# One layer of a hybrid encoder step: gate projections by seven products, gate and branch projections with the tokens stationary

## The chip, the core and the metric

The kernel runs on one core of one Trainium2 chip, as one launch. The metric is the device time of one execution in microseconds (us), median of several. Besides there is one profiled execution, whose trace and profile page are quoted here. Engines are named as in the profile: PE is TensorE (matmuls), DVE is VectorE, ACT is ScalarE, POOL is GpSimd, SP is SyncE; the last two mostly issue DMAs here.

## What is computed

384 tokens (256 of a new prompt, 8 x 16 of running streams) go through one layer with model width 2048; all is fp32.

```
u = rmsnorm(x);  P = u @ w_in            # columns: pool 2048 | z 4096 | x,B,C 6144 | dt 64 | gates a, b 2 x 2048
A = pooled(P.pool) per group @ pool_w * pool_scale      # windows 2, 4, 8, 16: mean minus self
B = gated_rmsnorm(ssd_scan(silu(conv(x,B,C)), dt) + D x, silu(z))
m = sigmoid(g_a) * (A @ w_pool_proj) + sigmoid(g_b) * (B @ w_ssd_proj)
x = x + rmsnorm(m @ w_out)
x = x + rmsnorm(relu(rmsnorm(x) @ w_up)^2 @ w_down)
```

New pool, conv and SSD states are outputs too.

## The kernel before

Every fp32 operand of a matmul is split into a high part (`h`, rounded to the short fp32 format of TensorE) and the rest (`l`); a product is then three matmuls, h by h, l by h and h by l, into one PSUM accumulator (`mm3`, L80 to L82). The split of a weight tile of 128 x 1024 is one ACT copy (L71) and one DVE subtraction (L73); activations are split in the same way. SP fetches the weight tiles (`wfetch`, L63, 512 KB each) into three buffers.

Most projections are written with the weights stationary: a tile of 128 output columns stays in the array and the 384 tokens move, so one matmul has 384 columns and the result lies with features on partitions and tokens along the free axis. `proj` runs over the k-tiles of such a tile, 16 for the input projections (`xgh`, `xgl`, the split normalised input without its per-token factor `rstd`), 32 for the SSD projection. The output projection `wo` and the MLP's down projection are written the other way (`moving`, `down_units`): 128 tokens are stationary, 512 weight columns move, and the result has tokens on partitions. The down projection already computes the 256 prompt tokens by Strassen's seven products over 2 x 2 blocks (tokens by k by columns) and the 128 stream tokens plainly; `down_units` forms the sums of weight blocks on DVE (L862), evicts its accumulators by ACT copies (L878), and adds them up in DRAM by accumulating POOL DMAs (L882).

The order of the work is that of the program text, except for the MLP, whose units are put in order by `run`:

1. Input tiles p0 to p15 of the pool branch (`pool_tile`: windows by shifted additions on DVE, L251), with the group maps (`pool_map`) between them.
2. Gate a and the pool product, tile by tile: `gate_a(n)`, then `proj` of `w_pp`, their product to DRAM (`ma_scr`). `dt_phase` stands behind the last map: a chain of small DVE and ACT instructions with its transposes (`tk`).
3. Eight SSD groups: six `conv` tiles, four z tiles, the scan's matmuls (its C by B product is `cb`, L461), results to DRAM (`a_scr`). After each of the first six groups comes one tile of gate b (`gate_b`), after the last group the other ten; each goes to DRAM (`gb_scr`).
4. The SSD projection, tile by tile over 32 k-tiles, with `a_scr` read back through three buffers (`ar`, L617) and split (`abh` L620, `abl` L621); the merged tile is formed with `ma_scr` and `gb_scr` (`mar`, `gbr`) and split into `mh`, `ml`.
5. `wo` (L652 to L654), second norm, MLP up and down.

PSUM has eight banks, four for `mmtile` and four for `sstile`, all through.

Of the kernel before, what the change touches and what calls it, by code (L numbers as in the profile page):

```python
# [17 lines left out]
NB = 8  # L18
# [9 lines left out]
NG = 6  # L28
# [6 lines left out]
def build(ctx, tc, io):  # L35
# [5 lines left out]
    psm = ctx.enter_context(tc.tile_pool(name="psm", bufs=4, space=PSUM))  # L41
    pss = ctx.enter_context(tc.tile_pool(name="pss", bufs=4, space=PSUM))
    dram = ctx.enter_context(tc.tile_pool(name="dram", bufs=1, space=DRAM))

    cst = consts.tile([P, 352], F32, name="cst")
    vec = consts.tile([P, V_END], F32, name="vec")
# [3 lines left out]
    def mmtile(name):  # L50
        return psm.tile([P, 512], F32, tag="mm", name=name)

    def sstile(name):
        return pss.tile([P, 512], F32, tag="ss", name=name)

    hold = [None, None]
# [4 lines left out]
    def wfetch(src, name):  # L61
        w = wpool.tile([P, 1024], F32, tag="w", name=f"w_{name}")
        sy.dma_start(w, src)  # L63
        return w, name

    def wsplit(f):
        w, name = f
        h = wpool.tile([P, 1024], F32R, tag="wh", name=f"wh_{name}")
        l = wpool.tile([P, 1024], F32R, tag="wl", name=f"wl_{name}")
        with behind(hold[0]):  # L70
            s.activation(h, w, AF.Copy)  # L71
        with behind(hold[1]):
            v.tensor_tensor(l, w, h.bitcast(F32), ALU.subtract)  # L73
        return h, l
# [16 lines left out]
    last = [None]  # L91

    def proj(units, rhs, name):
        o = mmtile(f"pj_{name}")[:, :T]
        for q, src in enumerate(units):
            half(o, q, wload(src, f"{name}_{q}"), rhs)
        return o
# [15 lines left out]
    def rms_bc(pool, sumsq, n, name, after=None):  # L113
# [5 lines left out]
        y = newton(pool, ms, [P, 3], name)  # L119
        dg = pool.tile([P, 3, P], F32, tag="dg", name=f"dg_{name}", bufs=1)  # L120
# [8 lines left out]
    ma_scr = [dram.tile([P, T], F32, name=f"ma_scr{i}") for i in range(16)]  # L129
    gb_scr = [dram.tile([P, T], F32, name=f"gb_scr{i}") for i in range(16)]  # L130
# [3 lines left out]
    dec_scr = dram.tile([NH, NB], F32, name="dec_scr")  # L134

# [37 lines left out]
    w = wpool.tile([P, 1024], F32, tag="w", name="w_p0_0")  # L173
# [37 lines left out]
    s.copy(rstd, rms_bc(pa, acc, DM, "x"))  # L211
    pha.close()

    small.tile([P, 88], F32, name="pad_small")
    tok = small.tile([P, 11, NH], F32, name="tok")
    decb = small.tile([P, NH, NB], F32, name="decb")
    with tc.tile_pool(name="phc", bufs=1, reuse_waits="tile") as pc, tc.tile_pool(name="phc2", bufs=2, reuse_waits="tile") as pc2:
        pst = pc.tile([P, KD, NB, 15], F32, name="pst")
        gp.dma_start(pst, io["state_pool"])
        bufs = []  # L220
        for i in range(2):
            b = pc.tile([P, 519], F32, name=f"pbuf{i}")
            gp.memset(b[:, :15], 0.0)
            bufs.append(b)
        A = [None] * KD
        dd = [[None] * 4 for _ in range(4)]

        def pool_tile(gi, k4):
            w = WINDOWS[gi]
            k = gi * 4 + k4  # L230
            ps = early[k] if k < 3 else proj(in_units(1 + k), xg, f"p{k}")
            bf = bufs[k % 2]
            pv = bf[:, 15:271]
            sv = bf[:, 271:].rearrange("p (b t) -> p b t", b=NB)
# [7 lines left out]
            s.copy(sv[:, :, :15], pst[:, k])  # L242
# [10 lines left out]
            d = pc2.tile([P, T], F32, tag="d", name=f"d{k}")  # L253
            v.scalar_tensor_tensor(
# [13 lines left out]
            h = pc2.tile([P, T], F32R, tag=f"dh{k4}", name=f"dh{k}", bufs=1)  # L268
            l = pc2.tile([P, T], F32R, tag=f"dl{k4}", name=f"dl{k}", bufs=1)
            s.activation(h, d, AF.Copy)  # L270
            v.tensor_tensor(l, d, h.bitcast(F32), ALU.subtract)
            dd[gi][k4] = (h, l)

        def pool_map(gi):
            for hf in range(2):
                h, l = wload(io["pool_w"][gi, hf], f"pw{gi}_{hf}")
                for n2 in range(2):
                    n = gi * 4 + hf * 2 + n2
                    o = mmtile(f"pw{n}")[:, :T]
                    for k in range(4):  # L280
                        c = slice((n2 * 4 + k) * P, (n2 * 4 + k + 1) * P)
                        mm3(o, h[:, c], l[:, c], dd[gi][k][0], dd[gi][k][1], k == 0, k == 3)
                    ah = pc.tile([P, T], F32R, name=f"ah{n}")
                    al = pc.tile([P, T], F32R, name=f"al{n}")
                    sc = vec[:, V_PSC + n : V_PSC + n + 1]
                    s.activation(ah, o, AF.Copy, scale=sc)
                    v.scalar_tensor_tensor(
                        out=al, in0=o, scalar=sc, in1=ah.bitcast(F32), op0=ALU.mult, op1=ALU.subtract
                    )
                    A[n] = (ah, al)  # L290

        def gate_a(n):
            ps = proj(in_units(17 + n), xg, f"ga{n}")
            t = pc2.tile([P, T], F32, tag="d", name=f"gat{n}")
            v.tensor_tensor(t, ps, rstd, ALU.mult)
            sg = pc2.tile([P, T], F32, tag="sg", name=f"gas{n}")
            s.activation(sg, t, AF.Sigmoid)
            return sg

        def dt_phase(pb):  # L300
            ps = proj(in_units(0), xg, "dt")
            n64 = lambda nm: pb.tile([NH, T], F32, name=nm)
            dtb = vec[:NH, V_DTB : V_DTB + 1]
            alog = vec[:NH, V_ALOG : V_ALOG + 1]
            nA = pb.tile([NH, 1], F32, name="nA")
            s.activation(nA, alog, AF.Exp)
            raw, ab, e, t1, t2, q = (n64(x) for x in ("raw", "ab", "e", "t1", "t2", "q"))
            v.tensor_tensor(raw, ps[:NH], rstd[:NH], ALU.mult)
            s.activation(ab, raw, AF.Abs, bias=dtb)
            s.activation(e, ab, AF.Exp, scale=-1.0)  # L310
            v.tensor_scalar(t1, e, 2.0, None, ALU.add)
            v.reciprocal(t2, t1)
            v.tensor_tensor(t1, e, t2, ALU.mult)
            v.tensor_tensor(t2, t1, t1, ALU.mult)
            v.tensor_scalar(q, t2, 1.0 / 19.0, None, ALU.mult)
            for i in range(8, 0, -1):
                v.scalar_tensor_tensor(out=q, in0=q, scalar=1.0 / (2 * i + 1), in1=t2, op0=ALU.add, op1=ALU.mult)
            v.scalar_tensor_tensor(out=q, in0=q, scalar=1.0, in1=t1, op0=ALU.add, op1=ALU.mult)
            v.tensor_scalar(raw, raw, dtb, 0.0, ALU.add, ALU.max)
            dt, cum = n64("dt"), n64("cum")  # L320
            v.scalar_tensor_tensor(out=dt, in0=q, scalar=2.0, in1=raw, op0=ALU.mult, op1=ALU.add)
            dta, we, dtw = n64("dta"), n64("we"), n64("dtw")
            v.tensor_scalar(dta, dt, nA, -1.0, ALU.mult, ALU.mult)
            v.tensor_tensor_scan(cum, cst2[:NH, C_SCAN - C_MASK : C_SCAN - C_MASK + T], dta, 0.0, ALU.mult, ALU.add)
            sy.dma_start(cum_scr, cum)
            nb = n64("nb")
            tot = pb.tile([NH, 1], F32, name="tot")
            v.tensor_tensor(tot, cum[:, 127:128], cum[:, 255:256], ALU.add)
            v.tensor_scalar(nb[:, :P], cum[:, :P], cum[:, 127:128], -1.0, ALU.subtract, ALU.mult)
            v.tensor_scalar(we[:, :P], cum[:, :P], tot, -1.0, ALU.subtract, ALU.mult)  # L330
            v.tensor_scalar(we[:, P:TP], cum[:, P:TP], cum[:, 255:256], -1.0, ALU.subtract, ALU.mult)
            cs = cum[:, TP:].rearrange("h (b t) -> h b t", b=NB)
            last = cs[:, :, TS_ - 1 : TS_]
            v.tensor_tensor(
                we[:, TP:].rearrange("h (b t) -> h b t", b=NB), last.to_broadcast([NH, NB, TS_]), cs, ALU.subtract
            )
            s.activation(we, we, AF.Exp)
            v.tensor_tensor(dtw, dt, we, ALU.mult)
            s.activation(nb[:, TP:], cum[:, TP:], AF.Exp)
            dec = pb.tile([NH, NB], F32, name="dec")  # L340
            s.activation(dec, last.squeeze(2), AF.Exp)
            sy.dma_start(dec_scr, dec)
            sy.dma_start(decb, dec_scr.partition_broadcast(P))
            srcs = [cum[:, i * P : i * P + P] for i in range(3)] + [dt[:, i * P : i * P + P] for i in range(3)]
            srcs += [dtw[:, i * P : i * P + P] for i in range(3)] + [nb[:, :P], nb[:, TP:]]
            for r in range(2):
                part = srcs[r * 8 : r * 8 + 8]
                o = sstile(f"tk{r}")
                for i, a in enumerate(part):
                    te.transpose(o[:, i * NH : i * NH + NH], a, ident[:NH, :NH])  # L350
# [4 lines left out]
        for gi in range(4):  # L355
            for k4 in range(4):
                pool_tile(gi, k4)
                if gi and k4 == 0:
                    pool_map(gi - 1)
# [824 lines left out]
```

## Time and profile before

| | |
|---|---|
| device time, median of 3 runs | 2840.26 us (2840.02 to 2841.51) |
| profiled execution | 2840.66 us |
| its span in the trace | 2838.9 us |
| matmul records | 15997 |
| granted TensorE clock, mean | 0.996 |
| bytes moved by DMA | 492.90 MB, mean 174 GB/s |

A group row of the profile reads: line, engine, operation, output <- input by the program's names, partitions x elements, how often; then the busy time in us, the mean duration in ns, and how long the engine sat idle before it, with what ended that. In a timeline row the first number is the start, the second the duration. A window row has, after the window and its length, the busy time of each engine, the granted clock, the mean busy share of the 16 DMA engines and the GB/s they moved. A DMA row ends with the KB of one transfer and the median time from issue to landing. Matmul durations overlap, so the time that one costs is the distance from start to start.

### The profile page before, as it was taken

The page shows a single profiled execution, that of the slowest core. Times are in us where ns is not written, and L with a number is a line of the kernel's source. Part 1 is how long each engine was busy: PE and PEld are TensorE (multiplying, and loading weights), DVE is VectorE, ACT ScalarE, POOL GpSimd, SP SyncE. Part 2 cuts the span into 40 slices and gives each one's busy share as a digit, 9 for nine tenths or more (in the row PEclk, how much of TensorE's full clock was granted, in tenths as well). Part 3 has the DMA queues.
Part 4 walks back from the last instruction along what each step waited for, and adds up shares of the span by engine and source line. Part 5 has one row for each costly group of instructions (what it writes and reads, how often), then busy time and mean ns, then how long its engine had stood idle before and what let it go on. Part 6 is the DMA issues. An engine that isn't in the chain of part 4 may idle for free.

```text
span 2838.9 us, 40540 instructions
## 1 busy us (share of the span) xinstructions
PE 2811.2 (99%) x15997; PEld 2655.9 (94%) x15997; DVE 1798.0 (63%) x2501; ACT 1280.2 (45%) x1869; POOL 254.8 (9%) x324
## 2 busy tenths in 40 slices
PE   9999999999999999999999999999999999999997
PEld 8999999999999999999999988899999999999996
DVE  7774335678678677677533333666767667676766
ACT  5443224445345445443522223545555455555543
POOL 0000000011011011011000000000111111111121
PEclk9999999999999999999999999999999999999999
DMA  6444445456465465465744453445666566666654
GB/s 215 132 135 138 138 141 194 146 202 215 151 212 200 155 221 189 161 232 189 240 149 154 149 182 130 151 164 189 184 167 163 160 164 158 180 183 186 175 157 195
DMA packets 160784, 492.90 MB, mean 174 GB/s; under 512 B 19809, under 2 KB 43553, under 8 KB 155729
## 3 DMA queue, kind: packets, MB, share of 16 engines
q1 hardware_dynamic: 133296, 410.14, 42.5%
q0 software_dynamic: 27296, 80.18, 11.6%
q8 instruction: 125, 2.05, 0.3%
q14 instruction: 67, 0.54, 0.1%
HBM read 412.34 MB, written 77.89 MB: 173 GB/s over the span
## 4 chain that ended last, share of the span: by engine, by line
PE 97%; DVE 1%; ACT 0%; issue 0%; DVEq 0%; ACTq 0%
PE pj_up L80 6%; PE pj_up L81 6%; PE pj_up L82 6%; PE pj_x L82 5%; PE pj_x L80 5%; PE pj_x L81 5%; PE wd L914 3%; PE pj_sp L80 3%; PE wd L916 3%; PE wd L915 3%; PE pj_z L82 3%; PE pj_z L80 3%; PE pj_sp L81 3%; PE pj_z L81 3%; PE pj_sp L82 3%; PE t L914 2%
## 5 line engine op out<-in xcount | busy, mean ns | idle before, releaser
L80 PE MATMUL pj_up<-x1h,wh_up 128*128 128x384 f32 x1024 | 345.6, 338 | 0.0
L81 PE MATMUL pj_up<-x1l,wh_up 128*128 128x384 f32 x1024 | 345.2, 337 | 0.0
L82 PE MATMUL pj_up<-x1h,wl_up 128*128 128x384 f32 x1024 | 344.7, 337 | 0.0
L80 PE MATMUL pj_x<-xgh,wh_x 128*128 128x384 f32 x768 | 261.4, 340 | 0.0
L82 PE MATMUL pj_x<-xgh,wl_x 128*128 128x384 f32 x768 | 258.3, 336 | 0.0
L81 PE MATMUL pj_x<-xgl,wh_x 128*128 128x384 f32 x768 | 256.8, 334 | 0.0
L73 DVE TENSOR_TENSOR wl_wd<-raw,wh_wd 128x1024 fp32r<-128x1024 f32 x168 | 202.3, 1222 | 68.8 <-ACT wh_wd L71 66.9
L71 ACT ACTIVATE wh_wd<-raw 128x1024 fp32r<-128x1024 f32 x168 | 175.1, 1054 | 96.9 <-PE pj_up L81 84.2
L80 PEld LDWEIGHTS pj_up<-x1h,wh_up 128*128 128x128 f32 x1024 | 192.8, 188 | 4.8 <-ACT x1h L732 0.4
L81 PEld LDWEIGHTS pj_up<-x1l,wh_up 128*128 128x128 f32 x1024 | 192.8, 188 | 4.5
L82 PEld LDWEIGHTS pj_up<-x1h,wl_up 128*128 128x128 f32 x1024 | 192.8, 188 | 0.1
L82 PE MATMUL pj_z<-xgh,wl_z 128*128 128x384 f32 x512 | 171.0, 334 | 0.0
L80 PE MATMUL pj_z<-xgh,wh_z 128*128 128x384 f32 x512 | 171.0, 334 | 0.0
L82 PE MATMUL pj_sp<-abh,wl_sp 128*128 128x384 f32 x512 | 171.0, 334 | 0.0
L81 PE MATMUL pj_z<-xgl,wh_z 128*128 128x384 f32 x512 | 171.0, 334 | 0.0
L80 PE MATMUL pj_sp<-abh,wh_sp 128*128 128x384 f32 x512 | 171.0, 334 | 0.0
L81 PE MATMUL pj_sp<-abl,wh_sp 128*128 128x384 f32 x512 | 171.0, 334 | 0.0
L73 DVE TENSOR_TENSOR wl_sp<-w_sp,wh_sp 128x1024 fp32r<-128x1024 f32 x64 | 78.3, 1224 | 118.9 <-ACT wh_sp L71 118.1
L882 POOL DMA_DIRECT2D acc_scr<-ev x108 | 92.7, 928 | 667.5 <-ACT ev L878 650.6
L80 PEld LDWEIGHTS pj_x<-xgh,wh_x 128*128 128x128 f32 x768 | 144.3, 188 | 2.5 <-issue 1.4
L82 PEld LDWEIGHTS pj_x<-xgh,wl_x 128*128 128x128 f32 x768 | 144.2, 188 | 2.6 <-issue 2.6
L81 PEld LDWEIGHTS pj_x<-xgl,wh_x 128*128 128x128 f32 x768 | 144.3, 188 | 1.1 <-issue 0.2
(335 smaller groups left out, 7112.4 us busy)
## 6 DMA issues: line engine op xcount, KB each, us to landing
w_up<-w_up SPq DMA_DIRECT2D x128, 512.0 KB, 4.4
raw<-w_down SPq DMA_DIRECT2D x112, 512.0 KB, 7.3
w_x<-w_in SPq DMA_DIRECT2D x96, 512.0 KB, 3.8
w_z<-w_in SPq DMA_DIRECT2D x64, 512.0 KB, 3.5
w_sp<-w_ssd SPq DMA_DIRECT2D x64, 512.0 KB, 3.5
acc_scr<-ev POOLq DMA_DIRECT2D x126, 256.0 KB, 4.6
w_ga<-w_in SPq DMA_DIRECT2D x32, 512.0 KB, 3.5
w_pp<-w_pp SPq DMA_DIRECT2D x32, 512.0 KB, 3.4
```

Source lines behind the costliest of these rows:

```text
L71: s.activation(h, w, AF.Copy)
L73: v.tensor_tensor(l, w, h.bitcast(F32), ALU.subtract)
L80: te.matmul(out, wh, xh, start=first, stop=False)
L81: te.matmul(out, wh, xl, start=False, stop=False)
L82: return te.matmul(out, wl, xh, start=False, stop=last)
L882: gp.dma_start(acc_scr[p][r], e, accum_op=ALU.add)
L914: te.matmul(o, ah, wh[:, c], start=first, stop=False)
L915: te.matmul(o, ah, wl[:, c], start=False, stop=False)
L916: te.matmul(o, al, wh[:, c], start=False, stop=fin)
```

## The change

- Gate a and the first half of gate b (three halves of 1024 columns) are computed by seven products for the prompt tokens and plainly for the stream tokens, over two halves of k. `fast_units` is the former `down_units`, generalised; the sums of token blocks come from a fresh load of x (`x_sums`). The nine accumulators of each half go to DRAM (`seven`), the second k half accumulating.
- These 96 units are woven with the pool tiles p6 to p15, the maps 1 to 3 and the pool product, in one sequence that `run` executes in a written order (`evenly`, `weave`, weights beside each filling unit). PSUM is split there into 3 banks for `mmtile`, 2 for the stream tokens' accumulators and 3 for `pl` (maps and pool product); weight tiles arrive in two buffers.
- The pool product has tokens stationary (32 units of 18 matmuls) and goes to DRAM as `pp_scr`. `dt_phase` follows the whole sequence. The SSD groups have no gate tiles.
- The second half of gate b and the SSD projection use `moving`: 2 x 8 and 4 x 16 units of 18 matmuls. The sigmoid takes the per-token factor as its scale.
- `merge_pair` loads the nine products of one half, forms the four gate quadrants on DVE, applies the sigmoid and writes them to `ma_scr` or `gb_scr`; it is called inside the first two column blocks of the SSD projection. `gather` and `weigh` load the gate and the pool product and multiply them. All these loads and stores go through POOL's queue.
- `ar` has two buffers in place of three. At the end of a column block `merged` loads `gbr` and finishes three tiles of 128 tokens x 512, and 12 transposes bring them to the layout that `wo` takes (`mh`, `ml`).

```diff
-    def proj ... gate_a / gate_b ... w_pp by proj ... (stages 2 to 4 above)
+    def fast_gates(kb, ahead=None):
+        out = []
+        for p in range(3):
+            out += fast_units(
+                f"f{kb}_{p}", [io["w_fast"][kb, p, i] for i in range(4)],
+                lambda k, b: [y[:, b * P : b * P + P] for y in xg[kb * 8 + k]],
+                xsum, "t2",
+                lambda r, o, p=p: m1_away(seven[p][r], o, kb == 0, f"f{kb}_{p}_{r}"), ...
+    split = mixed(tiles, pp0[:8])
+    first = [(6, None, after, False)] + with_maps(1) + split + pp0[8:]
+    turn_ = with_maps(2) + tiles2[:2]
+    second = tiles2[2:] + [(9, None, [], False)] + with_maps(3) + pp1
+    units += evenly(fast0[:44], first) + evenly(fast0[44:], turn_) + evenly(fast1, second)
...
+    with tc.manual_schedule():
+        banks(mm=3, t2=2, pl=3)
+        rest()
...
-            if g < NG:
-                gate_b()
-        while gates:
-            gate_b()
...
-    with ... tc.tile_pool(name="phe2", bufs=3, reuse_waits="tile") as pe2:
+    pe2 = branch.enter_context(tc.tile_pool(name="phe2", bufs=2, reuse_waits="tile"))
...
+    def merge_pair(p, at, begin, sink):
+        def load(*rs):
+            def go():
+                for r in rs:
+                    got[r] = pe2.tile([P, 512], F32, tag="sv", name=f"sv{p}_{r}", bufs=9)
+                    gp.dma_start(got[r], seven[p][r])
...
+        def add(o, x, y):
+            with behind(mark[0]):
+                v.tensor_tensor(o, x, y, ALU.add)
...
+        for k, f in zip((0, 3, 4), (load(0, 1, 5, 6, 3, 4, 2, 7, 8), first, second)):
+            at.setdefault(begin + k, []).append(f)
+    for nb in range(2):
+        if nb:
+            branches(0, 0, 16)
+        o = [mmtile(f"gb{nb}_{b}") for b in range(3)]
+        moving(o, [(io["w_gb"][nb, kp], f"gb{nb}_{kp}") for kp in range(8)], xg, 0, gated)
+    main.close()
+    branches(1, 16, 32)
+    banks(mm=6, ss=2)
+    for nb in range(4):
+        o = [mmtile(f"sp{nb}_{b}") for b in range(3)]
+        mtok, at = [], {}
+        if nb < 2:
+            merge_pair(nb, at, 1, lambda i: ma_scr[2 * nb + i])
+        if nb == 0:
+            merge_pair(2, at, 6, lambda i: gb_scr[i])
...
+        def merged(b):
+            ma = mtok[b][0]
+            gb = pe2.tile([P, 512], F32, tag="gbr", name=f"gbr{nb}_{b}", bufs=2)
+            gp.dma_start(gb, gb_scr[nb][b])
+            v.tensor_tensor(gb, o[b], gb, ALU.mult)
+            v.tensor_tensor(ma, ma, gb, ALU.add)
+        moving(o, [(io["w_ssd"][nb, q], f"sp{nb}_{q}") for q in range(16)], ab, 0, merged, at)
+        for kk in range(4):
+            tr = sstile(f"trs{n}")
+            for b in range(3):
+                te.transpose(tr[:, b * P : b * P + P], mtok[b][0][:, kk * P : kk * P + P], ident)
```

More of the change, by code (lines that the diff above doesn't have):

```diff
@@ L292, in gate_a @@
[L292 to L350, printed above, removed]
-                v.tensor_copy(
-                    tok[:, r * 8 : r * 8 + len(part), :].rearrange("p a h -> p (a h)"), o[:, : len(part) * NH]
-                )
@@ L371, in build @@
+    tok = late.tile([P, 11, NH], F32, name="tok")
+    decb = late.tile([P, NH, NB], F32, name="decb")
+    with tc.tile_pool(name="phdt", bufs=1, reuse_waits="tile") as pdt:
+        dt_phase(pdt)
     with tc.tile_pool(name="phd", bufs=2, reuse_waits="tile") as pd, tc.tile_pool(
@@ L721, in build @@
     mpool.close()
+    banks(mm=4, ss=4)
     pga_hold = ExitStack()
@@ L1060, in build @@
     units += last
+    begin, rest = run(units)
     with tc.manual_schedule():
-        run(units)
+        begin()
+        rest()
 def _consts(np):
```

796 lines of the change are left out of this document (566 added, 230 removed).

## The prediction

> **What bounds the kernel now.** I read the page first, for the engine that is never free, then the timeline for what one matmul really takes, then the groups, the DMA rows and the windows for the engines and transfers that the new stages lean on.
>
> ```profile
> span 2838.9 us, 40540 instructions
> PE 2811.2 (99%) x15997; PEld 2655.9 (94%) x15997; DVE 1798.0 (63%) x2501; ACT 1280.2 (45%) x1869; POOL 254.8 (9%) x324
> PE 97%; DVE 1%; ACT 0%; issue 0%; DVEq 0%; ACTq 0%
> ```
>
> TensorE carries 97% of the chain that ended last; only 28 us of the span are without a matmul. So the kernel is worth the number of its matmuls times the interval from one start to the next, and every new wait of TensorE is added in full. The durations in the groups overlap, so the interval is read from start to start:
>
> ```profile
> 1549.72 0.33 PE L82 MATMUL pj_sp<-abh,wl_sp 128*128 128x384 f32 x1
> ...
> 1555.96 0.33 PE L82 MATMUL pj_sp<-abh,wl_sp 128*128 128x384 f32 x1
> ...
> 2411.90 0.39 PE L914 MATMUL wd<-wh_wd,sh 128*128 128x512 f32 x1
> ...
> 2414.39 0.39 PE L916 MATMUL wd<-wh_wd,sl 128*128 128x512 f32 x1
> ...
> 1699.79 0.39 PE L653 MATMUL wo<-wl_wo,mh 128*128 128x512 f32 x1
> ...
> 1711.92 0.39 PE L654 MATMUL wo<-wh_wo,ml 128*128 128x512 f32 x1
> ```
>
> 36 intervals in 6.24 us: a matmul with 384 columns takes 0.1733 us, its columns at 2.4 GHz (0.1600) and 13.3 ns. 11 intervals in 2.49 us and their neighbours: 512 columns take 0.2267 in the down stage (0.2133 and 13.3 ns). 52 intervals in 12.13 us: in the output projection the same shape takes 0.2333 (20 ns). What differs between the last two is where the stationary tile starts in SBUF: `mp`'s tiles lie 32 bytes past a multiple of 64, the down stage's on one.
>
> **The matmuls.** Gate a, gate b and the pool product lose 768 matmuls of 384 columns each, the SSD projection 1536: 3840 x 0.1733 = 665.6 us. Added, all with 512 columns: 576 for the pool product, 1152 for the SSD projection, 288 for the last half of gate b, 792 for three gate halves by seven products (504 with `xg` stationary, 288 with the token sums). By the addresses in the built program, `xg` starts at 32 past 64, so its 504 + 288 take 0.2333 (184.8 us); the other 2016 take 0.2267 (457.0 us). Together 641.8: 23.8 us less. With all at 0.2333 the saving would be 10.5, with all at 0.2267 29.0. Seven products account for only 72 of the 1032 matmuls fewer, about 16 us; the rest is the fixed 13.3 ns, paid less often.
>
> By the Trainium skill, "TensorE: Matmul & The Clock Gate", section "Wait — 56ns, not 53.3ns?", a warm matmul costs about 2.5 ns beyond its columns. The rows here say 13.3 to 20; by the page's figure, as an estimate, 3840 x 0.1625 less 2808 x 0.2158 would leave a saving of 18.0 us.
>
> The result of the SSD projection now has tokens on partitions, so 48 transposes of 128 columns come before the output projection:
>
> ```profile
> L480 PE MATMUL trx<-cst,xs 128*128 128x128 f32 x96 | 15.7, 273 | 0.0
> ```
>
> 15.7/96 = 0.16 us, 7.9 us for 48, all on TensorE. TensorE alone thus goes to 2840.7 - 23.8 + 7.9 = 2824.8 (from this execution's 2840.66, 0.4 above the median of the three runs).
>
> **The SSD stage without gates** removes matmuls counted above, and nothing else should move: a group with a gate starts its C by B product 108.3 us after the one before, the group without 100.1, and 48 x 0.1733 = 8.3 is the difference.
>
> ```profile
> L461 PE MATMUL cb<-xs,xs x6: 272/275/382, 1080.8 to 1081.5; 128*128 128x128 f32 x4, 128*128 128x256 f32 x2
> ...
> L461 PE MATMUL cb<-xs,xs x6: 272/275/382, 1189.1 to 1189.9; 128*128 128x128 f32 x4, 128*128 128x256 f32 x2
> ...
> L461 PE MATMUL cb<-xs,xs x6: 272/275/382, 1289.2 to 1290.0; 128*128 128x128 f32 x4, 128*128 128x256 f32 x2
> ```
>
> The dt chain moves from behind gate tiles to behind the first SSD tiles; its cover stays some 20 us. I cost it at nothing; with the cover 1 us short it would cost that 1.
>
> **The mixed stage (three gate halves, pool tiles, pool products).** Here a 1024-column weight half is used for only 6 or 12 matmuls where the pass is plain or once-used, not 24, so the engines that split weights come under load.
>
> ```profile
> L73 DVE TENSOR_TENSOR wl_wd<-raw,wh_wd 128x1024 fp32r<-128x1024 f32 x168 | 202.3, 1222 | 68.8 <-ACT wh_wd L71 66.9
> L71 ACT ACTIVATE wh_wd<-raw 128x1024 fp32r<-128x1024 f32 x168 | 175.1, 1054 | 96.9 <-PE pj_up L81 84.2
> L862 DVE TENSOR_TENSOR raw<-raw,raw 128x2048 f32<-128x2048 f32 x56 | 127.9, 2285 | 0.0
> L251 DVE TENSOR_TENSOR win<-pbuf 128x518 f32<-128x518 f32 x16 | 11.1, 697 | 0.4
> L878 ACT COPY ev<-wd 128x512 f32<-128x512 f32 x98 | 55.4, 566 | 0.0
> L621 DVE TENSOR_TENSOR abl<-ar,abh 128x384 fp32r<-128x384 f32 x32 | 16.9, 557 | 12.8 <-ACT abh L620 12.7
> L620 ACT ACTIVATE abh<-ar 128x384 fp32r<-128x384 f32 x32 | 16.1, 524 | 17.6 <-DMA ar<-a_scr 17.4
> ```
>
> First place: between the last pool tiles (p13 to p15, window 16, four adds each) and `pw3` no filling is left, and the second block's first gate units follow one another. By the order of the instructions DVE must do, from the low half of tile 12 to the split of `pw3_0`, 10 weight splits (12.2 us), 4 raw adds (9.1), 12 window adds (8.3), 4 low halves (2.2) and some 16 small pieces (about 4.6): 36.4 us. TensorE's matmuls between the end of p14 and `pw3_0` are 48 x 0.1733 and 84 x 0.2333 less the few at 0.2267: 27.7. DVE is 8.7 late; the small pieces may be shorter than I put them, so 6 to 9: I take 8. Elsewhere in the stage DVE stays under TensorE.
>
> Second place: the pool product has three PSUM banks, and the next chunk opens the same three. ACT empties them with one 0.566 copy behind each following unit, and those copies queue behind the splits of these units. At the change from chunk 1 to 2 ACT has 5 splits and 5 copies, 5.3 + 2.8 = 8.1 us, until the third bank is free; TensorE has three short gate units of 6 matmuls and the first 6 of the new chunk, 4.2 + 1.4 = 5.6, 2.5 less. Seven such changes, 0.4 to 2.6 each by the same count: 8 us. Their bounds are 0 (filling longer than counted) and 14 (two each).
>
> **The SSD projection.** Before, its input came back from DRAM through three buffers, well ahead:
>
> ```profile
> L617 SPq DMA_DIRECT2D ar<-a_scr x32: 319/320/425, 1335.1 to 1396.3; - x32
> DMA to landing us min/median/max: 2.9/3.5/4.3
> ```
>
> Now there are two buffers, and SP issues two `ar` loads between two weight loads. A slot turns in 0.32 + 3.5 + 0.52 + 0.56 = 4.9 us, and so does the pair; a unit of 18 matmuls takes 4.08. The first load is issued about 22 us before the first unit needs it (behind the fetch of gb1_7), the sixteenth pair is needed 22 + 15 x 4.08 = 83 us after that issue and is there after 16 turns: up to a turn of 5.2 us nothing waits. That margin of 0.3 is what the rest has to fit into. For POOL's queue now brings 27 tiles of the seven products, their gated results go out and come back, and pool products come in: some 49 transfers of 256 KB in the same 83 us (12.8 MB), beside 16 weight tiles of 512 KB (8.4 MB) and 32 `ar` (6.3 MB): 27.5 MB, 331 GB/s.
>
> ```profile
> 1349.00:1420.00 71.00, 71.00 (x411) 71.00 (x411) 41.87 (x59) 36.55 (x56) 3.87 (x8) 1.00 0.72 238
> 2750.00:2770.00 20.00, 20.00 (x96) 17.27 (x95) 11.92 (x14) 7.79 (x9) 9.69 (x18) 1.00 0.97 344
> 2760.00:2780.00 20.00, 20.00 (x90) 16.55 (x89) 11.19 (x14) 7.17 (x11) 6.97 (x13) 1.00 1.04 427
> ...
> raw<-w_down SPq DMA_DIRECT2D x112, 512.0 KB, 7.3
> ...
> w_sp<-w_ssd SPq DMA_DIRECT2D x64, 512.0 KB, 3.5
> acc_scr<-ev POOLq DMA_DIRECT2D x126, 256.0 KB, 4.6
> ```
>
> The last two columns are DMA share and GB/s: at a share of 0.97 the engines moved 344 and at 1.04 (large plain copies) 427, so the ceiling lies between 355 and 411, and the new stretch asks for 81 to 93% of it, where the old one (238) stood at 0.72. The rows below say what that does: a 512 KB load lands after 3.5 us in the SSD projection and after 7.3 in the down stage. I take a landing of 4.6, some three tenths of the way from the one to the other, since the new stretch lies between the two in its share: a turn of 6.0, the last pair there after 16 x 6.0 = 96 us, 13 us late. Some 5 of these show already at the first unit, because ACT frees the accumulators of gb1 (their sigmoid) only behind `abh8`, the ninth load, and the projection opens that bank. The bounds are 0 (nothing is crowded) and 35 (landings of 6 us, turn 7.4). ACT and DVE are in order, so weight splits queued behind a late `ar` are late as well; that is how the wait reaches TensorE.
>
> At the ends of the four column blocks TensorE waits for the third merged tile, whose gate is loaded only once the first one's buffer is free: some 5 us after the block's end (4.6 by POOL's row above), while 20 matmuls (4.7 us) run. 0 to 1 each: 1 us.
>
> **Sum.** 2824.8 + 8 + 8 + 13 + 1 = 2855.
>
> **Rivals.** (1) Transfers aren't crowded: landings stay at 3.5 us, the turn at 4.9, and only the mixed stage's waits are left: 2824.8 + 16 + 1 = 2842, no change. For it: the window of 427 GB/s; against it that `ar` itself took up to 4.3 us at 238. The Trainium skill, "DMA: Bandwidth & Descriptors", section "Measured (HBM→SBUF, 128 partitions, SWDGE, issued from GpSimd)", has a single core at 425 GB/s; by that the stretch would be at 78% and this rival would hold. Only the one window of large copies comes near that here. (2) Crowding is worse: `ar` lands after 6 us, and ordered additions of gate tiles, which wait for POOL's loads, stand ahead of weight splits on DVE; 30 to 35 us in place of 13: 2872 to 2877, and further if the mixed stage's upper bounds come with it. For it the 7.3 us row; against it that SP's and POOL's queues share the engines, so a late POOL load gives room to SP. (3) Faster: in the mixed stage filling covers as meant (0 to 4 us of waits) and nothing is crowded: 2825 to 2832. It decides if DVE's 36 us were under 28, that is, if its instructions overlapped by a quarter; the raw adds alone speak against it. (4) That the change doesn't do what it says is excluded by the counts: 2808 matmuls replace 3840.
>
> **How the numbers follow.** Runs of this kernel tell 0.2% (5.7 us) from no change. The sum as told 0.50 (2846 to 2867); rival 1 0.22 (2833 to 2846); rival 2 0.17 (2867 to 2885); rival 3 0.11 (2822 to 2833). Faster takes rival 3 and a little of rival 1, 0.13; same the rest of rival 1, 0.20; slower 0.67. The range leaves out rival 3 and the upper half of rival 2: 2833 to 2876.
>
> **What would show it.** Right: intervals of 0.2333 in the gate units and 0.2267 in the SSD projection; PE idle of about 8 us before `pw3`, ended by DVE; pieces of about 1 us at the pool product's bank changes, ended by ACT; idle at the start and in the first column block of the SSD projection, ended by `abh` and weight splits whose own wait is the `ar` load; a DMA share over 0.9 there. Wrong: no idle in that first block, or a stage that starts late for a reason not named here, such as the conv state's load ahead of the SSD stage or the transposes.

## The result and the profile after

The changed kernel takes 2883.05 us (median of 4 runs, 2881.43 to 2885.89) beside 2840.7 for the kernel before on the same chip: 1.0149 times as long, 95% interval 1.0137 to 1.0162. The forecast was 2855, with a range of 2833 to 2876: the sign was right, and 28 us were missing. First the page of the changed kernel: span, busy engines, and the chain that ended last.

```profile
span 2880.9 us, 38992 instructions
PE 2823.8 (98%) x15013; PEld 2540.6 (88%) x15013; DVE 1910.9 (66%) x2599; ACT 1355.8 (47%) x1997; POOL 342.4 (12%) x464
PE 79%; issue 14%; POOL 2%; DMA 2%; DVE 1%; ACT 1%; SPq 0%; POOLq 0%; DVEq 0%; ACTq 0%
```

984 matmul records fewer (1032 less 48 transposes), and yet PE is busy 12.6 us longer. TensorE's idle time rose from 27.7 to 57.1 us, and TensorE carries 79% of the chain where it carried 97%. So there are two questions: which waits came, and why the matmuls that are left take longer.

**The waits.** TensorE's waits in the mixed stage (100 to 540 us), in the SSD projection's first block (1390 to 1480) and after it (1480 to 1760): who waited for whom, total us, times, longest.

```profile
PE pp L322 <- ACT ev_pp L305: 6.4, 9, 1.9
PE wdf L288 <- DVE wl_f L96: 5.2, 2, 4.8
PE pw L103 <- ACT ev_pp L305: 0.3, 1, 0.3
...
PE sp L335 <- ACT wh_sp L94: 6.5, 2, 3.8
PE sp L335 <- ACT gbt L1100: 6.0, 1, 6.0
PE sp L336 <- DVE wl_sp L96: 2.6, 3, 1.1
...
PE trs L1156 <- DVE mar L1146: 2.5, 4, 1.2
```

All four are at the places that the prediction named: the bank changes of the pool product (ended by the copies `ev_pp`), the stretch before `pw3` (ended by VectorE's `wl_f`), the start of the SSD projection (ended by the sigmoid `gbt`) with its first block, and the transposes. A wait row counts only what lies beyond the modelled end of the last matmul. Added up from start to start (transposes and the small matmuls of the scan left out), what exceeds the usual interval of a tile's matmuls by over 12 ns comes to 24.0 us before and 68.8 after: 45 us more, where the prediction had 30 for waits.

About 10 of these 45 us are not waits. Behind the longest waits the granted clock stands at half for a while, and the matmuls go on at that pace. Two rows of the SSD projection's start, and the window of five microseconds that they lie in (the last three columns are the granted clock, the DMA share and the GB/s):

```profile
1410.35 0.63 PE L336 MATMUL sp<-wl_sp,abh 128*128 128x512 f32 x1
...
1414.61 0.63 PE L337 MATMUL sp<-wh_sp,abl 128*128 128x512 f32 x1
...
1410.00:1415.00 5.00, 5.00 (x12) 3.88 (x13) 1.78 (x2) 2.60 (x5) 1.08 (x2) 0.50 0.94 304
```

Ten intervals take 4.26 us, 0.426 each instead of 0.227, and count as busy. The changed kernel has five such stretches that the kernel before lacks, of 3.4 or 6.8 us each (from 360.6, 490.3, 1408.4, 1446.0 and 1469.9 us on). Each lies in or right behind one of the five longest new waits, which take 2.1 to 6.2 us. So some 35 us of waits are left.

**The matmuls.** 56 matmuls in a row of an input projection, first and last, from the timeline of the kernel before and then of the changed one:

```profile
505.35 0.33 PE L80 MATMUL pj_z<-xgh,wh_z 128*128 128x384 f32 x1
...
514.89 0.33 PE L81 MATMUL pj_z<-xgl,wh_z 128*128 128x384 f32 x1
```

```profile
575.80 0.34 PE L103 MATMUL pj_z<-xgh,wh_z 128*128 128x384 f32 x1
...
585.51 0.34 PE L104 MATMUL pj_z<-xgl,wh_z 128*128 128x384 f32 x1
```

55 intervals take 9.54 us before (0.1735 us each) and 9.71 after (0.1765). Nothing in the change touches these instructions. The start of an SSD group shows it over 480 such matmuls; these are the rows of the C by B product in two windows of the changed kernel, each holding two groups:

```profile
L890 PE MATMUL cb<-xs,xs x12: 272/275/382, 610.0 to 712.2; 128*128 128x128 f32 x8, 128*128 128x256 f32 x4
...
L890 PE MATMUL cb<-xs,xs x12: 272/275/382, 711.4 to 813.6; 128*128 128x128 f32 x8, 128*128 128x256 f32 x4
```

711.4 - 610.0 = 101.4 us from group to group, where a group without a gate took 100.1 before. Over all 4656 matmuls with `xg` moving (the mean interval by tile is 176.1 to 177.1 ns in the changed kernel) 3 ns each make some 14 us. The matmuls of the up projection, with another moving operand, stayed at 173.5.

### The profile page after: what moved, and what is told of

Same layout as the page of the kernel before. It is cut to its first block, busy times and chain, and to the rows that moved or that the text cites. A ratio compares the mean times of both kernels' runs of the same rounds, so it can differ in the third digit from the quotient of the medians.

```text
span 2880.9 us, 38992 instructions
## 1 busy us (share of the span) xinstructions
PE 2823.8 (98%) x15013; PEld 2540.6 (88%) x15013; DVE 1910.9 (66%) x2599; ACT 1355.8 (47%) x1997; POOL 342.4 (12%) x464
## 4 chain that ended last, share of the span: by engine, by line
PE 79%; issue 14%; POOL 2%; DMA 2%; DVE 1%; ACT 1%; SPq 0%; POOLq 0%; DVEq 0%; ACTq 0%
PE pj_up L103 6%; PE pj_up L104 6%; PE pj_up L105 6%; PE pj_x L103 5%; PE pj_x L105 5%; PE pj_x L104 5%; PE pj_z L104 3%; PE pj_z L105 3%; PE pj_z L103 3%; PE wd L287 3%; PE wd L289 3%; PE wd L288 3%; PE t L287 2%; PE t L288 2%; PE t L289 2%
## 5 line engine op out<-in xcount | busy, mean ns | idle before, releaser
L96 DVE TENSOR_TENSOR wl<-raw,wh 128x1024 fp32r<-128x1024 f32 x168 | 201.9, 1223 | 62.7 <-ACT wh L94 58.5
L94 ACT ACTIVATE wh<-raw 128x1024 fp32r<-128x1024 f32 x168 | 174.2, 1053 | 84.5 <-PE pj_up L104 42.1
L94 ACT ACTIVATE wh_x<-w_x 128x1024 fp32r<-128x1024 f32 x96 | 101.7, 1059 | 154.1 <-issue 54.0
L103 PE MATMUL pj_z<-xgh,wh_z 128*128 128x384 f32 x512 | 173.4, 339 | 0.0
L104 PE MATMUL pj_z<-xgl,wh_z 128*128 128x384 f32 x512 | 173.4, 339 | 0.0
L105 PE MATMUL pj_z<-xgh,wl_z 128*128 128x384 f32 x512 | 173.3, 339 | 0.0
L335 PE MATMUL sp<-wh_sp,abh 128*128 128x512 f32 x384 | 152.7, 398 | 12.5 <-ACT wh_sp L94 6.5
L336 PE MATMUL sp<-wl_sp,abh 128*128 128x512 f32 x384 | 152.8, 398 | 2.6 <-DVE wl_sp L96 2.6
L337 PE MATMUL sp<-wh_sp,abl 128*128 128x512 f32 x384 | 152.1, 396 | 0.0
L96 DVE TENSOR_TENSOR wl_sp<-w_sp,wh_sp 128x1024 fp32r<-128x1024 f32 x64 | 78.4, 1225 | 110.2 <-ACT wh_sp L94 110.0
```

Source lines behind the costliest of these rows:

```text
L96: mark[0] = v.tensor_tensor(l, w, h.bitcast(F32), ALU.subtract)
L103: te.matmul(out, wh, xh, start=first, stop=False)
L104: te.matmul(out, wh, xl, start=False, stop=False)
L105: return te.matmul(out, wl, xh, start=False, stop=last)
L335: te.matmul(o[b], mh, wh[:, c], start=k == 0, stop=False)
L336: te.matmul(o[b], mh, wl[:, c], start=False, stop=False)
```

## The experiments

**What slows the matmuls with `xg`.** The change dropped a padding tile of 88 floats (`pad_small`) from the pool `small`, and put `tok` and `decb` elsewhere. By the addresses in the built programs, every `xg` tile started on a multiple of 512 bytes before and starts 96 bytes past one now. Two runs change only that padding. Here and below, ratios are to the kernel before on the same chip, which took 2840.7 to 2841.5 us there in the median.

```diff
 # e1_align: the changed kernel          # e2_before_shift: the kernel before
+    small.tile([P, 8], F32, ...)        -    small.tile([P, 88], F32, name="pad_small")
                                         +    small.tile([P, 64], F32, name="pad_small")
```

> The changed kernel with 32 bytes of padding ahead of xg, so that its tiles start on a multiple of 64 bytes again, as before the change (the tiles now start 32 past one). Theory A (the place of xg in SBUF): every matmul of 384 columns that moves xg falls from about 176.6 ns to 173.3 (4656 of them, 15 us), those of 512 columns with xg stationary from 233 to 227 ns (792, 5 us): 2883 - 20 = about 2863 us. Rival (the SSD stage is slower for another reason: other weight buffers, DMA traffic, load on ACT and DVE): intervals stay at 176 to 177 ns and the time within 3 us of 2883.

> The kernel before with its padding changed from 88 to 64 floats, which slides xg by 96 bytes, to 32 past a multiple of 64, and changes nothing else. Theory A: 6192 matmuls of 384 columns that move xg (pool tiles, gates a and b, dt, x and z) take 3.3 ns more: 2840.5 + 20.6 = 2861 us. Rival: 2840 to 2842 us.

e1_align, with `xg` 64 past a multiple of 512, took 2869.55 us (ratio to before 1.0101, 1.0084 to 1.0117), 13.5 less than the changed kernel. e2_before_shift, 96 past, took 2859.36 (1.0064, 1.0049 to 1.0079), 17.8 more than the kernel before, with no other edit (the group maps' 192 matmuls `pw` went from 173.4 to 175.7 ns with it; the projections without `xg` stayed). The same 56 matmuls in e2_before_shift and in e1_align:

```profile
510.84 0.34 PE L80 MATMUL pj_z<-xgh,wh_z 128*128 128x384 f32 x1
...
520.56 0.34 PE L81 MATMUL pj_z<-xgl,wh_z 128*128 128x384 f32 x1
```

```profile
572.60 0.34 PE L103 MATMUL pj_z<-xgh,wh_z 128*128 128x384 f32 x1
...
582.13 0.34 PE L104 MATMUL pj_z<-xgl,wh_z 128*128 128x384 f32 x1
```

9.72 us for 55 intervals in the one (0.1767), 9.53 in the other (0.1733). So the address alone is worth 13 to 18 us. But e1_align fell short of its expectation by 6 us, 5 of them because `xg` as stationary operand stayed slow: 41 matmuls of the gate projection, in e1_align and then in e5_xg512, where `xg` starts on a multiple of 512 again (24 floats of padding).

```profile
1362.76 0.40 PE L335 MATMUL gb<-wh_gb,xgh 128*128 128x512 f32 x1
...
1372.09 0.40 PE L336 MATMUL gb<-wl_gb,xgh 128*128 128x512 f32 x1
```

```profile
1358.44 0.39 PE L335 MATMUL gb<-wh_gb,xgh 128*128 128x512 f32 x1
...
1367.53 0.39 PE L336 MATMUL gb<-wl_gb,xgh 128*128 128x512 f32 x1
```

0.2333 us each at 64 past 512, 0.2273 at 0. The prediction's explanation of the slow 0.2333 (a start 32 past a multiple of 64) is refuted by e1_align; a start on a multiple of 512 takes it away.

```diff
 # e5_xg512 and e7_xg_mh512                       # e6_xg480
+    small.tile([P, 24], F32, ...)                +    small.tile([P, 32], F32, ...)
 # e7_xg_mh512 and, in the kernel before, e10_before_mh512: ahead of the pool mp
+    mpool.enter_context(tc.tile_pool(name="mpad", bufs=1, side="right")).tile([P, 120], F32, name="pad_m")
```

> The changed kernel with 24 floats of padding ahead of the token tiles, so that each row of xg starts on a multiple of 512 bytes (96 past one in the changed kernel, 64 past one in the run with 8 floats of padding). Theory A, a stationary row of 512 bytes that does not start on a multiple of 512 costs 6.7 ns: the 792 matmuls of 512 columns with xg stationary (384 in the gate projection, 408 of the products t_f) fall from 233.4 to 226.7 ns, so 5.3 us below the 8-float run's 2869.5: 2864. Theory B, xg as stationary operand is slower for another reason (its place in the pool, or its double use): those stay at 233.4 and the time stays 2869.5. Both: moving xg stays at 173.3 to 173.8.

> The changed kernel with 32 floats of padding: rows of xg start 480 bytes past a multiple of 512, which is 32 past a multiple of 64, as in the changed kernel (96 past 512). Theory A, a moving row that does not start on a multiple of 64 bytes costs 3 ns: pj_x, pj_z and pj_p stay at 176.7 and the time stays 2883. Theory B, only some offsets within 512 are slow (x1h, moving in the up projection, starts at 480 and takes 173.6): 173.5 ns and 2869.5. Both expect 233.4 ns for xg as stationary operand.

> As the run with 24 floats of padding, and 120 floats of padding ahead of the tiles mh and ml of the out projection, which start 480 bytes past a multiple of 512 in the changed kernel and before. Theory A (stationary rows off a multiple of 512 bytes cost 6.7 ns): the 576 matmuls of wo fall from 233.3 to 226.7 ns, 3.9 us more: 2860. Theory B (another reason): wo stays at 233.3 and the time is that of the 24-float run.

> The kernel before with 120 floats of padding ahead of the tiles mh and ml, so that they start on a multiple of 512 bytes instead of 480 past one; nothing else. Theory A (stationary rows off a multiple of 512 bytes cost 6.7 ns): the 576 matmuls of wo fall from 233.4 to 226.7 ns: 2840.8 - 3.9 = 2837. Theory B (the out projection's matmuls of the kernel before are paced by something else): 2841.

e5_xg512: 2865.88 us (1.0088, 1.0073 to 1.0103), theory A. e6_xg480: 2870.31 (1.0103, 1.0088 to 1.0118), `pj_z` at 0.1733 and the gate projection at 0.2333: theory B, 480 past 512 doesn't hurt the moving operand. e7_xg_mh512 took 2864.77 (1.0084, 1.0067 to 1.0101), only 1.1 below e5_xg512 instead of 3.9, although its 576 matmuls of `wo` did go from 233.3 to 226.9 ns on the mean; the runs of either kernel spread over 2.4 us. The kernel before shows it without that noise: e10_before_mh512, with `mh` and `ml` moved by 120 floats, takes 2837.21 us (0.9986, 0.9976 to 0.9995), 3.8 less, as theory A had it. 53 matmuls of its output projection:

```profile
1655.85 0.39 PE L653 MATMUL wo<-wh_wo,mh 128*128 128x512 f32 x1
...
1667.67 0.39 PE L654 MATMUL wo<-wl_wo,mh 128*128 128x512 f32 x1
```

11.82 us for 52 intervals, 0.2273, where the kernel before had 0.2333 (12.13). Last, one run with all offsets at once:

```diff
 # e9_offsets: between the pairs of token tiles
+            if k:
+                xgp.tile([P, 8], F32, name=f"pad_xg{k}")
             h = xgp.tile([P, T], F32R, name=f"xgh{k}")
```

> The changed kernel with 24 floats of padding and 8 more floats between the pairs of token tiles, so that xg 0 starts 32 bytes past a multiple of 512, xg 1 at 64, xg 2 at 96 and so on in steps of 32, xg 15 at 0. Each start offset is then seen in one run, as moving operand of 384 columns (pj_x, pj_z, pj_p, dt) and as stationary operand (gb, t_f). Stationary, both theories: all but xg 15 at 233.4 ns, xg 15 at 226.7 (5.0 us over the 24-float run). Moving, theory A (the start within 512 bytes decides, and 96 is one of a few slow places: 0, 64 and 480 were fast in the runs before this one): the matmuls of xg 2 at 176.7, of most others at 173.5; time 2865.9 + 5.0 + 1 to 3 = 2872 to 2874. Theory B (what was slow at 96 is not the place of the one row but how the whole set lies against the weights' buffers): no tile stands out, all near 173.5 or all near 176.7: 2871 or 2885.

2875.03 us (1.0121, 1.0106 to 1.0136). The gate projection's nine matmuls with `xg` 6 (224 past 512) and with `xg` 7 (256 past), first and last of each:

```profile
1375.65 0.40 PE L335 MATMUL gb<-wh_gb,xgh 128*128 128x512 f32 x1
...
1377.52 0.39 PE L337 MATMUL gb<-wh_gb,xgl 128*128 128x512 f32 x1
1377.75 0.39 PE L335 MATMUL gb<-wh_gb,xgh 128*128 128x512 f32 x1
...
1379.56 0.40 PE L337 MATMUL gb<-wh_gb,xgl 128*128 128x512 f32 x1
```

8 intervals in 1.87 us, then 8 in 1.81. Worked out in the same way for every tile (moving: 117 to 171 undisturbed intervals of `pj_x`, `pj_z` and `pj_dt` each; stationary: 8 intervals):

| start modulo 256 bytes | 0 | 32 | 64 | 96 | 128 | 160 | 192 | 224 |
|---|---|---|---|---|---|---|---|---|
| moving, ns (tiles at 0 to 224) | 175.3 | 173.3 | 174.8 | 176.2 | 173.8 | 176.8 | 176.4 | 174.8 |
| moving, ns (tiles 256 further) | 175.6 | 173.5 | 175.0 | 176.3 | 173.8 | 177.2 | 176.5 | 174.9 |
| stationary, ns (tiles 256 further) | 226.8 | 232.5 | 233.9 | 233.2 | 232.4 | 233.6 | 230.2 | 233.6 |

Both rows of the moving operand agree, so the pattern repeats every 256 bytes, not 512. Of these starts, in steps of 32 bytes, a stationary row is fast only on a multiple of 256. Theory A was right that the place of the row decides, and wrong that few places are slow. For the moving operand the neighbours count too: with all tiles at 64 or at 480 (224 past 256) the interval is 173.3, and in this mixture such tiles take 174.8. An interval belongs to two matmuls, and which of them it is put down to shifts a moving entry by up to 1.5 ns; the period of 256 stays. What happens inside the chip stays open.

**The SSD projection.** Two runs on the changed kernel: the 27 `sv` tiles set to a constant instead of loaded, and three `ar` buffers instead of two.

```diff
 # e3_no_sv_loads
-                    gp.dma_start(got[r], seven[p][r])
+                    gp.memset(got[r], 0.0)
 # e4_three_ar (the smaller cst makes room)
-    cst = consts.tile([P, 352], F32, name="cst")
+    cst = consts.tile([P, 288], F32, name="cst")
-    pe2 = branch.enter_context(tc.tile_pool(name="phe2", bufs=2, reuse_waits="tile"))
+    pe2 = branch.enter_context(tc.tile_pool(name="phe2", bufs=3, reuse_waits="tile"))
```

> The changed kernel without the loads of the seven products' results: the 27 tiles are zeroed by POOL in place of the DMAs, so the three gate halves come out as constants; all instructions of the other engines and all other DMAs stay. Theory B (crowded transfers): without these 7 MB the ar loads land after 3.5 us or less, and TensorE's waits at the start and in the first column block of the SSD projection (18 us) fall to 5 or less: about 2869 us. Rival (the two ar buffers set the pace whatever else moves): waits stay above 12 us, 2877 us or more.

> The changed kernel with three buffers for ar in place of two, as before the change (room from an unused part of the constants tile). Theory B (crowding): the third buffer lets a load start earlier but the same bytes wait for the same DMA engines: 0 to 3 us less, 2880 to 2883 us. Rival (slots): the turn falls from two loads in 6 us to three in 6.5, the waits of 18 us fall by 10 or more: 2873 us or less.

TensorE's waits from 1375 to 1476 us in e3_no_sv_loads, then in e4_three_ar:

```profile
PE sp L336 <- DVE wl_sp L96: 4.7, 7, 1.4
PE sp L335 <- ACT wh_sp L94: 1.3, 2, 0.7
PE sp L335 <- ACT gbt L1100: 1.1, 1, 1.1
```

```profile
PE sp L335 <- ACT gbt L1100: 8.0, 1, 8.0
PE sp L335 <- ACT wh_sp L94: 4.6, 2, 2.6
PE sp L336 <- DVE wl_sp L96: 1.5, 2, 0.8
...
```

Without the loads: 2869.82 us (1.0101, 1.0086 to 1.0116), 13.2 less, and the wait for the sigmoid is 1.1 instead of 6.0. Some 6 of the 13.2 are the three stretches at half clock, which are gone: from 1400 to 1470 us the granted clock is 1.00 here, where the changed kernel has 0.93.

```profile
1400.00:1470.00 70.00, 62.88 (x263) 48.42 (x262) 41.54 (x58) 36.37 (x55) 19.97 (x39) 1.00 0.76 250
```

With a third buffer alone: 2884.58 (1.0153, 1.0138 to 1.0168), nothing gained. So it is the transfers, not the slots. The rows of `ar` say how: issue to landing, in the changed kernel and then without the `sv` loads.

```profile
DMA to landing us min/median/max: 2.3/4.4/8.1
```

```profile
DMA to landing us min/median/max: 2.3/3.7/5.8
```

The first nine `sv` loads wait for no work of another engine and go out from 1379.2 to 1385.0 us, just when `ar` fills its first pairs; the later ones wait for a free slot. The median landing was forecast well (4.6 against 4.4); it is the longest ones that stop TensorE. The loads could also have hurt through VectorE, whose additions wait for `sv` ahead of weight splits. From 1380 to 1480 us VectorE stood only 1.2 us for `sv`, while ScalarE, which makes `wh_sp`, stood for `ar` (changed kernel, then without the loads):

```profile
ACT abh L1044 <- DMA ar<-a_scr: 44.0, 18, 5.0
```

```profile
ACT abh L1044 <- DMA ar<-a_scr: 31.0, 18, 3.7
```

**Both stretches rebuilt.** e11_drains is e7_xg_mh512 with the pool stage changed; e8_rebuilt has the SSD projection changed as well.

```diff
 # e11_drains and e8_rebuilt: three copies as one task, more fast products between blocks
-  (3.4 if kp == 0 else 2, u, [lambda ..., b=b: drain(nb, o, b) for b in range(3)] if kp == 3 else [], kp == 0)
+  (4.6 if kp == 0 else 2, u, [lambda ...: [drain(nb, o, b) for b in range(3)]] if kp == 3 else [], kp == 0)
 # e8_rebuilt: sv loads spread and paced by VectorE; column blocks 2, 3, 0, 1; one pair per block
+                    with behind(mark[0]):
+                        v.memset(got[r][:, :1], 0.0)
                     gp.dma_start(got[r], seven[p][r])
-        for k, f in zip((0, 3, 4), (load(0, 1, 5, 6, 3, 4, 2, 7, 8), first, second)):
+        for k, f in zip((0, 1, 2, 3, 4, 6, 7), (load(0, 1), load(5, 6), load(3, 4), load(2, 7), load(8), first, second)):
-  bufs=2 for "ar", 9 for "sv"
+  bufs=3 for "ar", 8 for "sv"
-            branches(0, 0, 16)
+            branches(0, 0, 8)          # 8 to 15 behind gb1's last sigmoid on ScalarE
-    for nb in range(4):
+    for pos, nb in enumerate((2, 3, 0, 1)):
+        if pos < 3: merge_pair((1, 0, 2)[pos], at, 4 if pos == 0 else 2, ...)
...
-  moving(o, [... for kp in range(8)], ms_, ...)                       # wo, in the order of the blocks
+  moving(o, [... for kp in (4, 5, 6, 7, 0, 1, 2, 3)], ms_, ...)
```

> As the run with both paddings (2864.8), and of the rebuilt version only the pool stage: the three copies that free the banks of one column block of the pool product together after the next unit of fast products, and a weight of 4.6 for a block's first unit instead of 3.4. Theory A: the waits before the next block's first matmuls (0.95, 0.87, 1.36, 1.62, 0.99, 0.87, 0.65, 0.86 and 2.36 us, 10.5 in all) go: 2854 to 2856; the 17 us that the rebuilt version gained beyond that come from the SSD projection. Theory B (VectorE paces the mixed stage and waits come back before pw3): 2862 to 2865.

> As the run with both paddings, and the two stretches of waits taken apart. SSD projection: column blocks in the order 2, 3, 0, 1, one pair of gate halves merged per block instead of two in block 0 and one in blocks 0 and 1; each sv load is preceded by a one-column memset on VectorE, so that two are issued per unit instead of nine at once; 8 sv and 3 ar buffers; the sigmoids of the last gate block ahead of abh8 on ScalarE. Pool stage: the three copies that free the banks of one column block of the pool product are issued together after the next unit of fast products, not one after each of three, and the weight of the first unit of a block is 4.6 instead of 3.4, which puts more fast products between two blocks. Theory A (crowded transfers cost the SSD projection some 17 us and bank changes the pool stage some 12): gaps of the SSD projection fall to 3 to 6 us and those of the bank changes to under 1.5, the DVE-bound wait of 5 to 6 us before pw3 stays: 2832 to 2838, under the kernel before. Theory B (the transfers or VectorE are at their limit whatever the order; waits come back in the later column blocks or in the next stage): 2848 to 2858.

e11_drains: 2851.03 us (1.0036, 1.0023 to 1.0049), 13.7 below e7_xg_mh512. Its waits in the mixed stage:

```profile
PE wdf L288 <- DVE wl_f L96: 5.3, 1, 5.3
PE pw L103 <- ACT ev_pp L305: 0.3, 1, 0.3
```

The nine waits of `pp` for `ev_pp` are gone, and nothing came back before `pw3`. e8_rebuilt: 2836.69 us (0.9986, 0.9977 to 0.9995), 14.3 below e11_drains, and the fastest version with the change. Its span and engines, and the waits from 1375 to 1476:

```profile
span 2834.5 us, 39037 instructions
PE 2793.9 (99%) x15013; PEld 2524.1 (89%) x15013; DVE 1910.4 (67%) x2626; ACT 1356.6 (48%) x1997; POOL 342.4 (12%) x464
```

```profile
PE sp L336 <- DVE wl_sp L96: 1.9, 3, 0.8
PE sp L335 <- ACT wh_sp L94: 0.8, 1, 0.8
PE sp L336 <- DVE sv L1059: 0.8, 1, 0.8
...
```

Theory A both times, e11_drains 3 us below its range. Which of e8_rebuilt's edits of the SSD projection won how much isn't shown; in its trace `ar` is through by 1416.7 us, where the changed kernel issues the last load at 1472.7. It beats the kernel before by 4.1 us, but that kernel wins as much by its own padding (e10_before_mh512, 2837.21): with all starts in place, the change as rebuilt and the kernel before are the same within 0.2%.

**The stretch before `pw3`.** Three of VectorE's 2048-column sums given to GpSimd, on e8_rebuilt.

```diff
 # e12_gpsimd_adds
-            v.tensor_tensor(raw[d], raw[d], raw[n], ALU.add)
+            (gp if nm == "f1_0" and d != "21" else v).tensor_tensor(raw[d], raw[d], raw[n], ALU.add)
```

> The rebuilt version (2836.7), and three of the four 2048-column sums of weights of the first gate half of the second half of the contraction are made by GpSimd instead of VectorE. Theory A (the 5.7 us wait before pw3 is VectorE's work, 36.4 us of it beside 27.7 us of matmuls): three sums of some 2.3 us leave VectorE ahead of it, the wait falls below 1.5 us: 2831 to 2833. Theory B (GpSimd needs 6 to 12 us a sum, worked out from 1.47 us for 512 and 2.26 us for 384 columns, and the splits that need the sums come late, or the two engines slow each other down): 2836 to 2845.

2839.92 us (0.9997, 0.9987 to 1.0006), 3.2 slower than e8_rebuilt; the wait for `wl_f` L96 grew from 5.3 to 6.8 us, another joined it, and the half clock there lasted 10.2 us instead of 3.4. Theory B, and the timeline of GpSimd and of VectorE shows which half of it:

```profile
339.18 5.23 POOL L242 TENSOR_TENSOR rawf<-rawf,rawf 128x2048 f32<-128x2048 f32 x1
349.38 4.58 POOL L242 TENSOR_TENSOR rawf<-rawf,rawf 128x2048 f32<-128x2048 f32 x1 [4.96 <-issue]
```

```profile
339.88 5.10 DVE L594 TENSOR_TENSOR win<-pbuf 128x518 f32<-128x518 f32 x1
349.70 5.35 DVE L174 TENSOR_TENSOR wl_f<-rawf,wh_f 128x1024 fp32r<-128x1024 f32 x1
```

A window addition of 0.69 us and a split of 1.22 us, as they are elsewhere, last over 5 us when they start beside a sum on GpSimd, and end 0.6 and 1.1 us after it, which is about their own length: VectorE stood still. The Trainium skill, "SBUF — State Buffer", section "SBUF: two separate sides", says that GpSimd and a VectorE instruction with two SBUF inputs take turns on one pair of ports, each for a whole instruction; these rows agree. A sum of 4.6 to 5.2 us on GpSimd then takes more from VectorE than the 2.3 us that it saves there.

## Why the prediction was wrong

- **The first step that failed** is the sentence that the SSD stage "removes matmuls counted above, and nothing else should move", and before it the use of one interval, 0.1733, for every matmul that the change doesn't touch. The prediction had read the new address of `xg` and priced it where `xg` is stationary; it didn't ask what it does where `xg` moves. That cost 13.5 us (e1_align) of the missing 28; the 1.3 us more per SSD group are there to be seen in the C by B rows.
- **The second step that failed** is that "every new wait of TensorE is added in full", at its own length and no more. Behind the longest waits the clock was at half, which cost some 10 us on top of 35 us of waits. The prediction has no term for it. That it follows from the waits is borne out by e3_no_sv_loads, where shorter waits in the SSD projection left no such stretch; no run changes a wait alone, and what decides a stretch's length isn't shown.
- **Matmuls.** 665.6 less 641.8: the counts are right, and so are 0.2333 for `xg` as stationary operand (233.8 to 234.2 ns measured) and 0.2267 in the SSD projection (227.1). The 288 matmuls with the token sums were priced at 0.2333 and took 0.2278 to 0.2294, 1 us less in all. The reason given for 0.2333 was wrong: it takes a start on a multiple of 256 bytes, not of 64. The 48 transposes were over-priced: 0.109 to 0.120 us from start to start, 5.5 us instead of 7.9.
- **Before `pw3`.** 8 us forecast, 5.2 in the wait rows, ended by VectorE as named, and over 2 more at half clock behind it. That the total comes near 8 is luck. TensorE waited for a gate unit ahead of `pw3`, and up to the end of that wait VectorE's timeline has 8 weight splits and 3 sums of weights, where the prediction counted 10 and 4. Giving such sums to GpSimd doesn't help (e12_gpsimd_adds).
- **Bank changes.** Mechanism and size were right: 8 us forecast, 8.8 from start to start and 1.6 at half clock. e11_drains gained 13.7, but only 9.5 of it at the pool product's intervals (9.9 us too long in e7_xg_mh512, 0.4 in e11_drains). Some 2 more are a shorter stretch at half clock before `pw3`; the rest lies in the SSD projection, which that edit doesn't touch.
- **SSD projection.** 13 forecast; from start to start 17.8 of waits and 5.8 at half clock. e8_rebuilt won 14.3 over e11_drains, and its first block still waits 3.5 us in its rows. The 5 us at its start by the sigmoid behind `abh8` were 6.0. That late `ar` loads reach TensorE through the weight splits queued behind them was right (the ScalarE rows above). The slots, which the forecast used to turn late landings into a delay of 13 us, don't matter (e4_three_ar); the loads do (e3_no_sv_loads). So the 13 came as near as it did by luck. Rival 1 fails with that: landings of up to 8.1 us came in this window of the changed kernel, at 286 GB/s and a share of 0.86, under the 0.9 that the prediction named as a sign of being right.

```profile
1400.00:1470.00 70.00, 54.97 (x218) 43.07 (x217) 35.61 (x50) 30.68 (x48) 19.07 (x36) 0.93 0.86 286
```

By the 425 GB/s of the Trainium skill, "DMA: Bandwidth & Descriptors", section "Measured (HBM→SBUF, 128 partitions, SWDGE, issued from GpSimd)", the stretch would have had room; in this trace the loads landed late all the same.

- **Transposes' waits.** 1 us forecast, 2.5 in the rows.
- **Rival 2** had the time, 2867 to 2885, but not the reason: it needed `ar` landings of 6 us, and their median was 4.4.

With the measured terms: 2840.7 - 23.8 + 5.5 + 45 of waits and half clock + 13.5 = 2881, 2 below the measurement. So the missing 28 us are 13.5 by the address, some 10 by matmuls at half clock, some 5 by waits that had been forecast too short, and 2.4 back from the transposes, with the rest unassigned.

## What to carry to other kernels

Where TensorE is the bound, an edit that only moves a tile in SBUF is an edit of the time: compare the start addresses of matmul operands before and after, and let 128-column stationary tiles of fp32 start on multiples of 256 bytes. A queue that waits for nothing sends its loads at once; what it crowds out stops TensorE by the slowest landing, not by the median. A small instruction on a paced engine ahead of each load spreads them, which was part of the rebuild that won 14 us here. A wait can cost more than its length: look at the granted clock behind it. Copies that free PSUM banks belong together, close behind the work that filled them, with other matmuls in between before the banks are needed again; e11_drains changed both at once.

## What the runs showed of the hardware that was not expected

- Moving operand, fp32 split, 384 columns: 173.3 ns from start to start with all tiles at 0, 64 or 480 past a multiple of 512 bytes, 176.7 with all at 96; in a mixture about 173 to 177, repeating every 256 bytes of the start.
- Stationary operand, 512 columns moving: 226.7 ns with the row's start on a multiple of 256 bytes, 230.2 at 192 and 232.4 to 233.9 at the others.
- VectorE's two-input instructions of 0.7 and 1.2 us took 5.1 and 5.35 us beside a GpSimd sum of 2048 columns, which itself took 4.6 to 5.2.
- Granted clock at half for 3.4 or 6.8 us in or behind waits of TensorE of 2.1 to 6.2 us: 512 columns took 0.426 us from start to start there, and five such stretches cost some 10 us in the changed kernel.
